# A token-major input replaced by a channel-major one in a hybrid mixer layer: no input transposes, norms by a column of ones, input loads on two queues

## The chip, the cores and the metric

The kernel runs on one core of a Trainium2 chip. That core has five engines, each with its own in-order instruction stream: TensorE (PE) for matrix products and transposes, VectorE (DVE) and ScalarE (ACT) for elementwise work and reductions, GpSimd (POOL), and SyncE (SP), which here only issues DMAs. ACT and POOL can issue DMAs too. The metric is device microseconds of one execution, as the median of several runs; lower is better. In the profile an instruction is named by its engine and by the line of the kernel file that made it.

## The reference

One layer reads 128 context tokens and 512 latent tokens of 1024 channels. The part that the change touches comes first in the layer: every token is divided by its root mean square, scaled and shifted by an adaLN modulation that depends on the group (context or latent), and sent through one input projection of 3840 columns.

```python
shift, scale, gate = jnp.split(silu(c) @ w_ada + b_ada, 3)
h = x * rsqrt(mean(x * x, -1) + EPS) * g_pre * (1 + scale) + shift
proj = h @ w_in            # 3840 columns: attention, HGRN2, Fourier, gates
```

The rest of the layer (neighbourhood attention with a position bias, a two-way gated linear recurrence, a Fourier mixing branch, the gates, the output projection, the post-norm and the residual) is the same before and after.

## The kernel before

All arithmetic is fp32. A large product is made from three fast ones: each operand is split into a rounded part `hi` and a remainder `lo` (`split`, line 129), and `mm3` (line 210) adds hi·hi, hi·lo and lo·hi in one PSUM bank. The 640 tokens (128 context, then 512 latent) are columns, handled in two halves of 320; the 1024 channels are eight groups `k` of 128, which lie on the partitions of `hT[0]` and `hT[1]` (the `hi` and the `lo` part of the modulated input `h`).

The start (`start_stream`, line 244) works like this. `load_x` (line 217) loads the input token-major: for each of five blocks of 128 tokens one tile `xa` of 640 channels and one tile `xb` of 384, ten DMAs on SP. `scale_x` (line 222) sums the squares of each token (ACT for `xa`, DVE for `xb`), takes square root and reciprocal, and multiplies both tiles by the result. Then comes a loop over the channel groups. For each `k`, `mod_cols` (line 195) multiplies two 512 KB blocks of the modulation weights `wss`, one for the scale and one for the shift, by the SiLU of the conditioning vectors (`csil`, line 171). The result is copied to `row` (line 266), transposed (line 270) and reduced to the columns `G` and `shift` (lines 272 to 275). `modulated` (line 233) then transposes the five 128x128 blocks of `x` that belong to channel group `k` on TensorE, lets ACT read them from PSUM with `G` as scale and `shift` as bias (lines 237 and 239), and lets DVE make the `hi` and `lo` parts (lines 240 and 241). `zf_stream` (line 283) follows with the twelve matmuls of that `k` for the first two projection blocks `zf0` and `zf1`; when all eight are in, `gate` (line 321) takes sigmoids on ACT.

What follows is one long sequence of projection blocks (`FILL`, line 30), the first of which is `zb0`, and in between the recurrences, the attentions, the Fourier branch and the output projection. A small planner (`Order`, line 39) interleaves these streams at trace time by estimated times, and a scheduler fixes each engine's order from that. SP's weight loads are chained: `load_raw` (line 175) and `load` (line 190) queue each behind the last weight load. `lb` and `lb1` (lines 153 to 160) are constants of the recurrence gate, computed before everything else, with an exponential on ACT. `sel` (line 147) is a constant that the output gates need late.

Of the kernel before, what the change touches and what calls it, by code (L numbers as in the profile page):

```python
# [71 lines left out]
def mixer_kernel(ctx: ExitStack, tc: tile.TileContext, A, O):  # L72
# [51 lines left out]

    def tr(out, src):
        od.now += 0.107
        last_tr[0] = te.transpose(out, src, ident).ins  # L127

    def split(src, hi, lo, hi_eng=None, lo_eng=None):
        (sc.copy if hi_eng is None else hi_eng.tensor_copy)(hi, src)  # L130
        (ve if lo_eng is None else lo_eng).tensor_sub(lo, src, hi.bitcast(F32))  # L131
# [19 lines left out]


    lb, lb1 = const("lb", [2, 2]), const("lb1", [2, 2])
    ve.tensor_sub(lb, lbl, lbl)
    sc.activation(lb, lb, ACT.Exp)
    ve.reciprocal(lb1, lb)
    ve.tensor_mul(lb, lb, lb1)
    ve.tensor_sub(lb, lb, lb)
    ve.tensor_scalar_max(lb, lb, 0.0)
    ve.tensor_scalar(lb1, lb, -1.0, 1.0, op0=ALU.mult, op1=ALU.add)  # L160
# [12 lines left out]
    wdma, nb = [], [1]  # L173
# [7 lines left out]
    def split_w(raw, lo_eng=None, shape=(KT, P), tags=("hi", "lo")):  # L181
        hi, lo = [wp.tile([P, *shape], F32R, tag=t, name=nm(t), bufs=WB[t]) for t in tags]
        split(raw, hi, lo, lo_eng=lo_eng)
# [11 lines left out]
    def mod_cols(out, w, chain):  # L195
# [8 lines left out]
    xa, xb = [T(tag="xa") for _ in range(5)], [T(384, tag="xb") for _ in range(5)]  # L204

    def xcols(i, k):
        return (xa[i] if k < 5 else xb[i])[:, k % 5 * P:k % 5 * P + P]
# [14 lines left out]
    def scale_x():  # L222
        for i in range(5):
            ss2 = S(2)
            sc.activation(T(), xa[i], ACT.Square, accum_out=ss2[:, 0:1])
            ve.tensor_tensor_reduce(PE_()[:, 0:384], xb[i], xb[i], 1.0, 0.0, op0=ALU.mult, op1=ALU.add,
                                    accum_out=ss2[:, 1:2])
            ve.tensor_add(rstd[:, i:i + 1], ss2[:, 0:1], ss2[:, 1:2])
# [902 lines left out]
```

## Time and profile before

| what | value |
|---|---|
| median of 3 runs (lowest to highest) | 435.74 us (435.19 to 435.88) |
| the profiled execution's own time | 436.31 us |
| its span, from first to last instruction | 434.5 us |
| busy PE / DVE / ACT / POOL | 410.3 / 303.2 / 204.7 / 7.4 us |
| instructions | 8311 |
| first matmul starts | 14.27 us |
| the chain that ended last: share on PE | 90% |

Busy time is the sum of the instructions' spans on an engine. Matmuls are pipelined, so two of them may overlap in a row of the timeline: the distance between two starts is what one costs, not its printed length. A row such as "idle before, releaser" says how long the engine sat idle just before an instruction and what ended that. The matmuls of `mod_cols` show as two records each, so one 512 KB block of modulation weights is x16 in the trace. "Slices" are fortieths of the span.

### The profile page before, as it was taken

Reading aid. Unit: us, or ns where it says so; the run is one execution under the profiler, and the core shown is the slowest. Engines: PE = TensorE matmul, PEld = TensorE weight load, DVE = VectorE, ACT = ScalarE, POOL = GpSimd, SP = SyncE. Lnnn points to the kernel's source line nnn. Section 1 sums busy time; section 2 is a strip of 40 time slices with the busy share of each in tenths; the row PEclk is TensorE's granted clock in tenths of the full one; section 3 lists DMA queues with packets and bytes.
Section 4 is the critical chain, followed back from the end, with each engine's and each line's share of the span. In section 5 each row is a group of like instructions: output and inputs, shape, how many; then the busy total and the mean of one; then the engine's idle time right before and its main releaser. Section 6 shows DMA issues by size and latency. Waiting matters only on the chain.

```text
span 434.5 us, 8311 instructions
## 1 busy us (share of the span) xinstructions
PE 410.3 (94%) x3176; PEld 373.0 (86%) x3176; DVE 303.2 (70%) x866; ACT 204.7 (47%) x546; POOL 7.4 (2%) x23
## 2 busy tenths in 40 slices
PE   0699999999998999999999999999999999999994
PEld 0388899999988998999899989899898889988884
DVE  2775479999986865885597658786679748471164
ACT  5524467575341525654454534744456553251231
POOL 2000000000020100000000000000000000000000
PEclk9999999999999999999999999999999999999999
DMA  7996143211202011132112423245324203245032
GB/s 241 411 407 228 49 154 116 66 55 50 84 23 74 13 60 50 56 97 66 40 61 67 146 67 92 93 152 181 100 55 141 98 1 105 76 160 205 0 146 98
DMA packets 19528, 47.62 MB, mean 110 GB/s; under 512 B 3184, under 2 KB 6912, under 8 KB 19488
## 3 DMA queue, kind: packets, MB, share of 16 engines
q1 hardware_dynamic: 19376, 46.94, 31.7%
q8 instruction: 25, 0.41, 0.4%
q0 software_dynamic: 112, 0.14, 0.3%
q14 instruction: 15, 0.12, 0.1%
HBM read 43.80 MB, written 3.28 MB: 108 GB/s over the span
## 4 chain that ended last, share of the span: by engine, by line
PE 90%; DVE 4%; DMA 3%; ACT 1%; issue 1%; SPq 0%; DVEq 0%; ACTq 0%
PE pb L113 83%; PE pb L127 6%; DMA vs<-wss 1%; DMA txa<-x 1%; DVE AL L451 1%; DVE t L525 1%; DVE AL L488 0%; ACT L681 0%; DVE lo L131 0%; DVE t L953 0%; ACT hi L130 0%; ACT pe L682 0%; DVE t L468 0%; DVE t L467 0%; DVE AC L451 0%
## 5 line engine op out<-in xcount | busy, mean ns | idle before, releaser
L113 PE MATMUL pb<-hT,hi 128*128 128x320 f32 x896 | 209.5, 317 | 3.0 <-DVE vs L131 1.5
L113 PEld LDWEIGHTS pb<-hT,hi 128*128 128x128 f32 x896 | 149.4, 188 | 9.5 <-issue 2.3
L113 PE MATMUL pb<-hT,lo 128*128 128x320 f32 x448 | 139.0, 312 | 0.0
L113 PEld LDWEIGHTS pb<-hT,lo 128*128 128x128 f32 x448 | 84.1, 188 | 1.0 <-DVE G L274 0.2
L131 DVE TENSOR_TENSOR lo<-raw,hi 128x1024 fp32r<-128x1024 f32 x35 | 42.8, 1223 | 26.9 <-ACT hi L130 26.5
L130 ACT CAST hi<-raw 128x1024 fp32r<-128x1024 f32 x35 | 36.8, 1051 | 41.9 <-PE pb L113 20.9
L113 PE MATMUL pb<-t,t 64*128 64x128 f32 (+2 forms) x414 | 43.1, 291 | 0.4 <-DVE AL L451 0.4
L113 PEld LDWEIGHTS pb<-t,t 64*128 64x128 f32 (+1 forms) x414 | 36.2, 188 | 4.8 <-issue 0.8
L130 ACT CAST pT<-pb 128x256 fp32r<-128x256 f32 x64 | 23.3, 372 | 19.3 <-DVE pT L131 12.3
L113 PE MATMUL pb<-hi,mh 128*128 128x512 f32 (+1 forms) x108 | 32.1, 376 | 0.0
L131 DVE TENSOR_TENSOR pT<-pb,pT 128x256 fp32r<-128x256 f32 x64 | 26.4, 418 | 1.7 <-ACT pT L130 1.5
L113 PEld LDWEIGHTS pb<-hi,mh 128*128 128x128 f32 x108 | 19.4, 189 | 3.2
L113 PE MATMUL pb<-pT,mh 128*128 128x512 f32 (+1 forms) x102 | 22.2, 364 | 0.0
L681 ACT ACTIVATE pe<-pb,s 128x256 f32<-128x256 f32 x32 | 15.3, 477 | 13.8 <-DVE s L680 7.9
L127 PE MATMUL pb<-ident,pe 128*128 128x128 f32 x136 | 20.9, 273 | 0.5 <-ACT pe L682 0.5
L113 PEld LDWEIGHTS pb<-pT,mh 128*128 128x128 f32 x102 | 17.7, 189 | 3.1
L936 ACT ACTIVATE t<-pb 128x512 f32<-128x512 f32 (+1 forms) x11 | 6.0, 551 | 30.1 <-PE pb L113 30.1
L113 PE MATMUL pb<-lo,mh 128*128 128x512 f32 (+1 forms) x54 | 20.2, 373 | 0.0
L127 PEld LDWEIGHTS pb<-ident,pe 128*128 128x128 f32 x136 | 16.6, 140 | 1.4 <-ACT pe L682 0.7
L451 DVE COPY_PREDICATED AL<-masks,pb 128x512 f32<-128x512 uint32 x24 | 16.5, 738 | 1.5 <-PE pb L113 1.5
L113 PE MATMUL pb<-pT,vs 128*128 128x256 f32 (+1 forms) x96 | 16.8, 321 | 0.0
L113 PE MATMUL pb<-vs,csil 128*32 128x128 f32 x64 | 3.3, 335 | 14.3 <-DMA vs<-wss 14.3
(205 smaller groups left out, 636.3 us busy)
## 6 DMA issues: line engine op xcount, KB each, us to landing
raw<-win SPq DMA_DIRECT2D x30, 512.0 KB, 3.5
pT<-wss SPq DMA_DIRECT2D x12, 512.0 KB, 10.2
raw<-wg SPq DMA_DIRECT2D x8, 512.0 KB, 3.5
raw<-wout SPq DMA_DIRECT2D x8, 512.0 KB, 3.5
t<-x SPq DMA_DIRECT2D x10, 256.0 KB, 6.1
o_y<-t SPq DMA_DIRECT2D x9, 256.0 KB, 2.1
vs<-wss SPq DMA_DIRECT2D x4, 512.0 KB, 9.3
tbl<-tbl SPq DMA_DIRECT2D x4, 512.0 KB, 3.5
```

Of the source, the lines that this page charges most:

```text
L113: return te.matmul(out, lhsT, rhs, start=start, stop=stop).ins
L127: last_tr[0] = te.transpose(out, src, ident).ins
L130: (sc.copy if hi_eng is None else hi_eng.tensor_copy)(hi, src)
L131: (ve if lo_eng is None else lo_eng).tensor_sub(lo, src, hi.bitcast(F32))
L451: ve.copy_predicated(out, mk.to_broadcast([P, i1 - i0, P]), src)
L525: ve.scalar_tensor_tensor(sall[r, cdst], sall[r, cs], Td[r, ip:ip + 1], pst[r, cdst], op0=ALU.mult, op1=ALU.add)
L681: sc.activation(pe[:, 256:512], ss[:, 256:512], ACT.Exp, bias=m[:, 1:2], accum_out=m[:, 3:4])
L936: sc.activation(T(512)[:, cs], po[:, 0:cs.stop - cs.start], ACT.Square, accum_out=ssb[:, j:j + 1])
```

## The change

The input gets a second layout in memory, `xT`: channels on the partitions, all 640 tokens along the free dimension, eight tiles of 128x640.

- Loads. The ten loads of `xa` and `xb` on SP go. Eight loads of `xT` tiles come, the even ones on SP and the odd ones on ACT's queue, as the first DMAs of the kernel. The conditioning vectors `cc` move from SP's front to ACT's queue, behind its four tiles; `lbl` moves to ACT's queue as well; `sel` moves from POOL's queue to SP's chain of loads, behind the weight loads of the first groups. The first weight load is now chained behind SP's last `xT` tile.
- Norms. ACT squares each `xT` tile and DVE adds the eight squares up. Five matmuls with a two-column block of ones add over the partitions, which leaves each token's sum on its partition. One square root and one reciprocal for all tokens follow, then five transposes of the result broadcast along a row, and two ACT copies: `rb` holds the inverse norm of every token on every partition. DVE multiplies each `xT` tile by `rb`, one tile per channel group.
- Modulation. The forty 128x128 transposes of `x` go; ACT reads the scaled `xT` tile from SBUF.
- Order. Edges (`turn`, `turn_names`) fix the order of some instructions on one engine: the modulation matmuls of group k+1 behind the row transposes of group k, DVE's `row` copy behind the last modulation step of the group before (for the first two groups behind its `lo` part of `hT`), the next multiplication by `rb` behind that copy, and the first weight splits behind `rb` and behind the first `h`.
- `lb` and `lb1` are computed after the `zf` matmuls, with their exponential behind the last `h` on ACT.

```diff
-    cc = const("cc", [KT, 2], dma=sy.dma_start)
-    lbl = const("lbl", [2, 2], dma=sy.dma_start)
+    xT = []
+    for k in range(KT):
+        xT.append(T(tag="xT"))
+        x_dma = (sc if k % 2 else sy).dma_start(xT[k], A["xT"][k]).ins
+        if k % 2 == 0:
+            x_last = x_dma
+    cc = const("cc", [KT, 2], dma=sc.dma_start)
...
-    sel = const("sel", [2, P])
+    ones = cp.tile([P, 2], F32, tag="ones", name="ones")
+    ve.memset(ones, 1.0)
...
-    wdma, nb = [], [1]
+    wdma, nb = [x_last], [1]
...
+            if k == 0 and prev is not None:
+                turn_names(chain[0], prev)
...
-    def load_x():
-        for i in range(5):
-            load(xa[i], A["x"][i * P:(i + 1) * P, 0:NT])
-            load(xb[i], A["x"][i * P:(i + 1) * P, NT:D])
-    def scale_x(): ...
+    def inverse_norms():
+        acc = T()
+        sc.activation(acc, xT[0], ACT.Square)
+        for k in range(1, KT):
+            sq = T()
+            sc.activation(sq, xT[k], ACT.Square)
+            ve.tensor_add(acc, acc, sq)
+        pn, pr = PB(), PB()
         for i in range(5):
+            mm(pn[:, 2 * i:2 * i + 2], acc[:, i * P:(i + 1) * P], ones)
+        sc.activation(rstd, pn[:, 0:10].rearrange(...)[:, :, 0], ACT.Sqrt, bias=eps, scale=1.0 / D)
+        ve.reciprocal(rstd, rstd)
+        for i in range(5):
+            tr((pr if i < 4 else pn)[:, i % 4 * P:i % 4 * P + P], rstd[:, i:i + 1].to_broadcast([P, P]))
+        rb = T()
+        sc.copy(rb[:, 0:512], pr)
+        return rb, sc.copy(rb[:, 512:NT], pn[:, 0:P])
-    def modulated(k, pm):
-        h, px = T(), PB()
-        for i in range(1, 5):
-            tr(px[:, (i - 1) * P:i * P], xcols(i, k))
-        sc.activation(h[:, P:NT], px, ACT.Identity, bias=shift[:, k, 1:2], scale=G[:, k, 1:2])
-        tr(pm[:, 384:512], xcols(0, k))
-        sc.activation(h[:, 0:P], pm[:, 384:512], ACT.Identity, bias=shift[:, k, 0:1], scale=G[:, k, 0:1])
+    def modulated(k):
+        h = T()
+        sc.activation(h[:, P:NT], xT[k][:, P:NT], ACT.Identity, bias=shift[:, k, 1:2], scale=G[:, k, 1:2])
+        h_act[0] = sc.activation(h[:, 0:P], xT[k][:, 0:P], ACT.Identity, bias=shift[:, k, 0:1], scale=G[:, k, 0:1])
...
-        scale_x()
+        rb, rb_act = inverse_norms()
+        ve.tensor_mul(xT[0], xT[0], rb)
...
-                mod_cols(pm[:, u * P:(u + 1) * P], raws[2 * k + u], [])
+                mod_cols(pm[:, u * P:(u + 1) * P], raws[2 * k + u], [], row_tr)
             yield 0
-            ve.tensor_copy(row, pm[:, 0:256])
+            row_copy = ve.tensor_copy(row, pm[:, 0:256])
+            if k:
+                turn(row_copy, row_done)
+            if k + 1 < KT:
+                turn(ve.tensor_mul(xT[k + 1], xT[k + 1], rb), row_copy)
...
+            row_tr = last_tr[0]
...
-            ve.tensor_scalar_add(shift[:, k, :], pt[:, 2:4], bss[:, k, 1:2])
-            modulated(k, pm)
+            row_done = ve.tensor_scalar_add(shift[:, k, :], pt[:, 2:4], bss[:, k, 1:2])
+            h_done = modulated(k)
             if k < 2:
-                zf_w.append(split_w(zraw[k]))
+                row_done = h_done
+            if k < 2:
+                zf_w.append(split_w(zraw[k], prev=rb_act))
+                rb_act = h_act[0]
...
+    lbl = const("lbl", [2, 2], dma=sc.dma_start)
+    def lower_bounds():
+        ve.tensor_sub(lb, lbl, lbl)
+        turn(sc.activation(lb, lb, ACT.Exp), h_act[0])
...
         for p in range(2):
             for u in range(2):
                 gate(p, 0, zf_acc[p][u][:, 0:320], u)
...
     def gate_vectors():
+        sel = const("sel", [2, P], dma=load)
```

In `zf_stream`, `lower_bounds()` is called between the last `zf` matmul and the four calls of `gate` shown above. On the host, `xT` is the transpose of `x`, cut into eight tiles; `x` itself stays as an input, since the residual at the end reads it.

More of the change, by code (lines that the diff above doesn't have):

```diff
@@ L123, in run_mm, with turn_names, turn @@
         chain.append(ins)
+    def turn_names(ins, prev):
+        tc.add_manual_dep(ins, prev.name, mybir.DependencyInfo(mybir.DependencyClass.NoSync, mybir.DependencyReason.DATA),
+                          reason="turns")
+    def turn(ins, prev):
+        turn_names(ins.ins, prev.ins)
+        return ins
     def tr(out, src):
@@ L127, in tr, with split @@
         last_tr[0] = te.transpose(out, src, ident).ins
-    def split(src, hi, lo, hi_eng=None, lo_eng=None):
-        (sc.copy if hi_eng is None else hi_eng.tensor_copy)(hi, src)
+    def split(src, hi, lo, hi_eng=None, lo_eng=None, prev=None):
+        ins = (sc.copy if hi_eng is None else hi_eng.tensor_copy)(hi, src)
+        if prev is not None:
+            turn(ins, prev)
         (ve if lo_eng is None else lo_eng).tensor_sub(lo, src, hi.bitcast(F32))
@@ L150, in mixer_kernel @@
     ve.memset(eps, EPS)
[L153 to L160, printed above, removed]
     def rsqrt_mean(ss, n):
@@ L179, in load_raw, with split_w @@
         return t
-    def split_w(raw, lo_eng=None, shape=(KT, P), tags=("hi", "lo")):
+    def split_w(raw, lo_eng=None, shape=(KT, P), tags=("hi", "lo"), prev=None):
         hi, lo = [wp.tile([P, *shape], F32R, tag=t, name=nm(t), bufs=WB[t]) for t in tags]
-        split(raw, hi, lo, lo_eng=lo_eng)
+        split(raw, hi, lo, lo_eng=lo_eng, prev=prev)
         return hi, lo
@@ L193, in load, with mod_cols @@
             sy.dma_start(t, src)
-    def mod_cols(out, w, chain):
+    def mod_cols(out, w, chain, prev=None):
         t = od.now
@@ L203, in mixer_kernel @@
     hT = [big.tile([P, KT, NT], F32R, tag=f"hT{j}", name=f"hT{j}") for j in range(2)]
-    xa, xb = [T(tag="xa") for _ in range(5)], [T(384, tag="xb") for _ in range(5)]
-    def xcols(i, k):
-        return (xa[i] if k < 5 else xb[i])[:, k % 5 * P:k % 5 * P + P]
     zf_w, zf_acc = [], [[PB("f"), PB("f")], [PB("f"), PB()]]
@@ L215, in mixer_kernel @@
     HF = (slice(0, 320), slice(320, 640))
-    def load_x():
+    def inverse_norms():
[6 more added lines that the diff above has]
+        pn, pr = PB(), PB()
         for i in range(5):
-            load(xa[i], A["x"][i * P:(i + 1) * P, 0:NT])
-            load(xb[i], A["x"][i * P:(i + 1) * P, NT:D])
-    def scale_x():
+            mm(pn[:, 2 * i:2 * i + 2], acc[:, i * P:(i + 1) * P], ones)
+        sc.activation(rstd, pn[:, 0:10].rearrange("p (i two) -> p i two", two=2)[:, :, 0], ACT.Sqrt, bias=eps, scale=1.0 / D)
+        ve.reciprocal(rstd, rstd)
@@ L223, in scale_x @@
         for i in range(5):
[L224 to L228, printed above, removed]
-            rsqrt_mean(rstd[:, i:i + 1], D)
-            ve.tensor_scalar(xa[i], xa[i], rstd[:, i:i + 1], 0.0, op0=ALU.mult, op1=ALU.add)
@@ L281, in start_stream @@
             yield max(0.0, 13.5 + 2.7 * (k + 1) - od.now)
+    lb, lb1 = const("lb", [2, 2]), const("lb1", [2, 2])
+    lbl = const("lbl", [2, 2], dma=sc.dma_start)
+    def lower_bounds():
+        ve.tensor_sub(lb, lbl, lbl)
+        turn(sc.activation(lb, lb, ACT.Exp), h_act[0])
+        ve.reciprocal(lb1, lb)
+        ve.tensor_mul(lb, lb, lb1)
+        ve.tensor_sub(lb, lb, lb)
+        ve.tensor_scalar_max(lb, lb, 0.0)
+        ve.tensor_scalar(lb1, lb, -1.0, 1.0, op0=ALU.mult, op1=ALU.add)
     def zf_stream():
@@ L290, in zf_stream @@
                 yield 0
+        lower_bounds()
         for p in range(2):
```

7 lines of the change are left out of this document (4 added, 3 removed).

## The prediction

> **What bounds the kernel now.** I read the page's busy shares first, then the waits of PE, then the busy time by stage, then the timeline of the first 55 us engine by engine.
>
> ```profile
> PE 410.3 (94%) x3176; PEld 373.0 (86%) x3176; DVE 303.2 (70%) x866; ACT 204.7 (47%) x546; POOL 7.4 (2%) x23
> ```
>
> The waits of PE over the whole span (us, times, longest), and the busy time by stage (stretch, its length, then busy time of PE, PEld, DVE, ACT, POOL with counts, the granted clock, the DMA engines' share, GB/s):
>
> ```profile
> PE pb L113 <- DMA vs<-wss: 14.3, 1, 14.3
> PE pb L113 <- DVE vs L131: 1.5, 1, 1.5
> PE pb L113 <- ACT t L326: 1.0, 1, 1.0
> ...
> 14.27:21.77 7.50, 7.30 (x75) 4.30 (x75) 5.09 (x17) 3.15 (x5) 0.00 (x0) 1.00 1.03 409
> ...
> 24.20:52.65 28.45, 28.45 (x337) 25.82 (x335) 16.29 (x49) 10.06 (x16) 0.00 (x0) 1.00 0.58 225
> ...
> 53.81:429.64 375.83, 371.99 (x2744) 340.99 (x2744) 271.57 (x767) 180.93 (x504) 4.33 (x12) 1.00 0.27 87
> ```
>
> PE waits once for 14.3 us, for its first weights, and then hardly at all: 372.0 of 375.8 us busy after the start. So whatever moves the instant 52.65, at which PE has finished the start's work, moves the rest rigidly; the change edits only what comes before it (and `sel` and `lb`, below). What fills PE from the first matmul on `h` (21.77, which I call T0) to 52.65:
>
> ```profile
> L113 PE MATMUL pb<-hT,hi 128*128 128x320 f32 x80 | 19.3, 327 | 0.1
> L113 PE MATMUL pb<-hT,lo 128*128 128x320 f32 x40 | 12.0, 314 | 0.0
> L113 PE MATMUL pb<-pT,csil 128*32 128x128 f32 x146 | 5.6, 277 | 0.0
> L127 PE MATMUL pb<-ident,txa 128*128 128x128 f32 x16 | 2.9, 283 | 0.0
> L127 PE MATMUL pb<-ident,row 128*128 128x128 f32 x14 | 2.8, 280 | 0.0
> L127 PE MATMUL pb<-ident,txb 128*128 128x128 f32 x15 | 2.5, 276 | 0.0
> L113 PE MATMUL pb<-vs,csil 128*32 128x128 f32 x48 | 2.2, 307 | 0.0
> ```
>
> Their real cost is the distance between starts (timeline of PE):
>
> ```profile
> 19.37 1.33 PE L127 MATMUL pb<-ident,txa 128*128 128x128 f32 x5
> 20.63 1.08 PE L113 MATMUL pb<-pT,csil 128*32 128x128 f32 x16
> 21.77 1.17 PE L113 MATMUL pb<-hT,hi 128*128 128x320 f32 x3
> ...
> 24.54 0.30 PE L113 MATMUL pb<-hT,lo 128*128 128x320 f32 x1
> 24.68 0.31 PE L113 MATMUL pb<-hT,hi 128*128 128x320 f32 x1
> ...
> 27.14 1.08 PE L113 MATMUL pb<-pT,csil 128*32 128x128 f32 x32
> 28.15 0.76 PE L127 MATMUL pb<-ident,txa 128*128 128x128 f32 x5
> ```
>
> From 24.5 on a 320-column matmul costs 0.147 us (24.54 to 24.68 and so on), five transposes about 0.73 (0.147 each), and the modulation of a whole group (x32) 1.01 us. Before that, all three cost about twice as much: one half of a group's modulation (x16) takes from 20.63 to 21.7, five transposes 1.26. So 120 x 0.147 = 17.6 us on `hT`, six groups of modulation 6.1, fourteen row transposes 2.1, thirty-one input transposes 4.6: 30.4 of the 30.9 us, the rest being the slow first pieces.
>
> **What goes.** Thirty-one of the forty input transposes lie in that full stretch: 4.6 us of PE, with nothing else to hide them. The other nine lie before T0, where PE is mostly waiting for the chain. DVE loses `scale_x`, ACT its five squares.
>
> **What T0 becomes.** Now the norms of all tokens hang on the last `xT` tile. The rows that bear on its arrival and on each link:
>
> ```profile
> 0.73 0.39 SPq L140 DMA_DIRECT2D cc<-cc  x1
> 1.65 0.42 SPq L193 DMA_DIRECT2D txa<-x  x1
> ...
> 2.00:10.70 8.70, 0.00 (x0) 0.00 (x0) 2.90 (x14) 4.90 (x11) 1.92 (x5) 1.00 0.93 293
> 6.00:7.00 1.00, 0.00 (x0) 0.00 (x0) 0.03 (x2) 0.00 (x0) 0.00 (x0) 1.00 1.01 272
> 10.00:36.00 26.00, 21.53 (x266) 16.28 (x267) 18.17 (x59) 10.80 (x23) 0.00 (x0) 1.00 1.03 407
> ...
> L541 ACT ACTIVATE t<-t 128x640 f32<-128x640 f32 x2 | 1.5, 737 | 0.1
> L424 DVE TENSOR_TENSOR t<-t,t 128x640 f32<-128x640 f32 x2 | 1.6, 818 | 0.0
> L113 PE MATMUL pb<-bones,t 128*128 128x2 f32 x20 | 2.5, 248 | 0.0
> L164 ACT ACTIVATE rstd<-rstd,eps 128x1 f32<-128x1 f32 x5 | 1.4, 288 | 1.3 <-DVE rstd L228 1.3
> L501 ACT COPY t<-pb 128x512 f32<-128x512 f32 x4 | 2.1, 589 | 8.3 <-PE pb L127 8.3
> L237 ACT ACTIVATE t<-pb,shift,G 128x512 f32<-128x512 f32 x8 | 6.2, 779 | 17.4 <-DVE G L274 17.4
> ...
> 21.22 0.49 DVE L240 CAST hT<-t 128x640 fp32r<-128x640 f32 x1 [1.60 <-ACT t L239]
> ```
>
> The ten loads are 2.62 MB (640 x 1024 x 4 bytes); at the 293 GB/s of the stretch they are in at about 10.9. The first `xT` load can be issued where `cc` was, at 0.73 instead of 1.65, 0.9 us earlier, with the same bytes: last tile at about 10.2 (with its receipt). Bounds: from 2.1 on, 407 GB/s would give 8.5 and 272 GB/s 11.7. Then: square 0.74; last add 0.82; five ones-matmuls, by the `bones` rows 0.63 and at the early pace twice that, 1.2; square root 0.29, its table load (1.28 elsewhere) behind add and matmuls; reciprocal 0.16; five transposes at the early pace 1.33; ACT copies 0.59 and about 0.3; multiplication 0.82; `h` in two ACT pieces 1.1; cast 0.49. Sum 7.8; with nine handoffs at 0.07 (the cast of 21.22 ends at 21.71, its matmul starts at 21.77) 8.5: T0 = 18.7. PE is in order and the first modulation weights land meanwhile, so one group at the early pace (two x16, 2.1 us) may stand between these small steps; I add 1.0. **T0 = 19.7**, bounds 17.0 (tiles at 8.5, nothing in between) and 25 (the first rival).
>
> On DMA a rule of the skill speaks against part of the change. The two-queue issue gets nothing from me but the 0.9 us start, because with one queue issuing the engines were already full (row 6.00 to 7.00 above: a share of 1.01).
>
> The Trainium skill, "DMA: Bandwidth & Descriptors", section "Issuing engines are not separate DMA queues", says that DMAs started by different engines run on the same 16 DMA engines and that only the time to issue is saved. The trace agrees as far as it goes; if the rule were wrong and two queues reached the 407 GB/s of later, the sum would gain 1.7 us.
>
> **From T0 to the end of the stage.** PE then has 17.6 + 6.1 + 2.1 = 25.8 us of work. Two things come on top. The early slow pace: it ended 2.4 us after T0 (24.2); I take 3 us at half speed, 1.5 us (bounds 0.5 and 4). And holes: the new edges make DVE's `row` copy of group 1 wait for `lo` of group 0, and put modulation k+1 behind row transposes k, so from group 2 on DVE paces the groups:
>
> ```profile
> L241 DVE TENSOR_TENSOR hT<-t,hT 128x640 fp32r<-128x640 f32 x8 | 6.6, 823 | 0.2
> L131 DVE TENSOR_TENSOR lo<-raw,hi 128x1024 fp32r<-128x1024 f32 x3 | 3.7, 1220 | 0.1
> L266 DVE COPY row<-pb 128x256 f32<-128x256 f32 x8 | 3.4, 421 | 1.6 <-PE pb L113 1.6
> L273 DVE TENSOR_SCALAR G<-s,bss 128x2 f32<-128x2 f32 x8 | 1.8, 227 | 0.2
> L272 DVE TENSOR_REDUCE s<-pb 128x4 f32<-128x16 f32 x8 | 1.4, 172 | 5.9 <-PE pb L127 5.9
> ```
>
> Back to back each starts about 0.08 before its printed end of the one before, so a group is 0.34 copy + 0.74 new multiplication + 0.10 reduce + 3 x 0.14 + 0.41 cast + 0.74 `lo` = 2.75 us. PE per group: 1.01 + 0.29 + 12 x 0.147 = 3.06. The two nearly balance, so holes come only near group 1, whose whole chain (copy, transposes, `G`, `h`, cast, `lo`) takes 4.8 us from T0 with 3 to 4 us of PE work to fill it: 1.5 us (bounds 0 and 3). End of the stage = T0 + 28.8 = 48.5, against 52.65: **4.1 us gained**. Weights do not bind: input, sixteen modulation blocks and two projection blocks are 12.1 MB, of which 2.55 were in at 10.7 and the rest follows at 407 GB/s, to 34 before and 33 after; the last group's chain behind them takes some 7 us, to 40.
>
> **What is moved.** `cc` arrives at about 10 instead of 3 us; its only reader is the SiLU for modulation, which needs weights that land later, unless ACT's order makes others wait (first rival). The exponential of `lb` with its own table goes from ACT's first idle microseconds to between the last `h` and the sigmoids:
>
> ```profile
> 0.73 1.28 ACT L155 ACT_TABLE_LOAD   x1 [0.73 <-PEq L1124]
> ...
> 51.70 1.28 ACT L325 ACT_TABLE_LOAD   x1 [2.08 <-PE pb L113]
> ```
>
> ACT sat idle 2.08 us there, which covers 1.28 + 0.2; uncovered it would cost up to 1.5. The sigmoids' own load, and with it PE's 1.0 us wait, stays. `sel` (128 KB) joins SP's chain, 0.3 us of DMA where weights are ahead of PE; `lbl` is 2 KB; memset, ones and DVE's seven adds (0.82 each) lie in the wait for the tiles. All of this I cost at nothing.
>
> Against the profiled execution's 436.31 us (434.5 us of span and 1.8 around it) this gives 432.2; the median of the runs is 0.57 lower, so **431.6 us**.
>
> **The rivals.** All but the last are priced by end = T0 + 28.8; T0 = 23.9 gives no gain at all.
>
> *ACT's queue blocks the norms (slower).* `cc` is issued fifth on ACT behind 1.3 MB of tiles. If the scheduler puts its SiLU ahead of the squares, ACT sits until about 10.4, then needs eight squares at about 0.65 apart before the last add: 15.6 instead of 10.9, T0 = 24.4; and all modulation from group 2 on hangs behind T0 by the new edges, so that nothing is done ahead meanwhile. The end is 53.2, with holes of 3 us 54.7: 436.3 to 437.8, taken at 437. For: ACT ran this SiLU before its first square in the trace. Against: the tiles land one by one, so squares are ready first. If only some squares stand behind, T0 is about 22 and the time 434.
>
> *DVE takes over.* If in-order waits add 1.0 us to its 2.75, the groups come 3.75 us apart: 4.8 for group 1, five more groups 18.8, two weight splits 2.3, and 4.9 from the last `row` copy to the last `zf` matmul make T0 + 30.8 = 50.5: 433.6. For: DVE's chain has no slack once it paces. Against: DVE was busy 16.3 of 28.45 us there, and the addition is 8 x 0.74.
>
> *The slow pace lasts.* PE has less to do before T0, and before, the fast pace came only 10 us after the first matmul although PE was busy 7.30 of 7.50 us. If it comes 8 us after T0, 4 instead of 1.5 us are lost: 434.1. The Trainium skill, "TensorE: Matmul & The Clock Gate", Part 1, says that the array runs at half clock until a busy window of about 3.4 us has passed. The trace agrees with the factor of two, not with the time: 24.5 is 10 us after the first matmul.
>
> *Everything goes well.* Tiles at 8.5, nothing between the small steps, no holes, an early pace that ends after 1 us: T0 = 17.0, end 43.3, 426.4; with half of that, 429.0.
>
> **How the numbers follow.** Forecast (429.0 to 433.5) 0.56; more gain 0.06; slow pace or DVE 0.14 (to 434.5); part of the squares blocked 0.09, of which a third is no change; norms blocked altogether 0.15, of which 0.03 within 0.2% and 0.12 slower. About 0.2% (0.9 us) is what a measurement can tell from no change. Faster 0.82, same 0.06, slower 0.12. For 8 in 10 the range is 428.8 to 435.4.
>
> **What would show it.** First matmul on `hT` near 19.7; no transposes of the input; the multiplications by `rb` at 0.82 us; PE full from about 24 to 48.5; the sigmoids' table load near 47.5; from there all rows 4 us earlier and the same. Wrong if squares start after 10 us, if T0 is past 23.9, if PE shows long waits between groups 1 and 3, or if later stages lose what the start gains (their order on the engines is set by the same scheduler, and I take it as unchanged).

## The result, and the profile after

The changed kernel is slower: 440.55 us in the median (439.01 to 441.72, 4 runs) against 435.47 (434.78 to 435.88) for the kernel before on the same chip, a ratio of 1.012 with an interval of 1.010 to 1.014. The forecast was 431.6, range 428.8 to 435.4. Measured a second time (below) it took 439.18, a ratio of 1.008; the two intervals do not overlap, and what made the first occasion slower by another 1.4 us is not known. Both are slower, where the forecast was faster. The profiled execution of the changed kernel took 439.01 us, with a span of 437.0; everything below is read from it against the profiled 436.31 and 434.5 of before.

The busy row of the page of the changed kernel, and the row of its PE matmuls on `bones`, a matmul far behind the start, with first and last start at the end of the row:

```profile
PE 408.7 (94%) x3151; PEld 372.7 (85%) x3151; DVE 306.7 (70%) x853; ACT 206.3 (47%) x542; POOL 7.6 (2%) x22
```

```profile
L113 PE MATMUL pb<-bones,t x20: 168/251/272, 122.8 to 146.0; 128*128 128x2 f32 x20
```

The same row of the kernel before:

```profile
L113 PE MATMUL pb<-bones,t x20: 168/251/272, 120.7 to 144.0; 128*128 128x2 f32 x20
```

PE has 1.6 us less to do and yet comes to `bones` 2.1 us later, and to its last matmul 2.04 us later (430.33 against 428.29). So the difference that the two profiles show arises ahead of this row, and the rest is shifted rigidly, as forecast, only in the other direction. (The spans of the profiles differ by 2.5 us, the medians by 5.1 and 3.5; the first experiment takes this up.) Span less first `bones` row is 313.8 us before and 314.2 after, and it lies between 313.8 and 314.4 in every run of this study. This row therefore serves as the mark of lateness below.

The waits of PE in the first 60 us of the changed kernel (us, times, longest), and the busy time by stage (stretch, length, busy time of PE, PEld, DVE, ACT, POOL with counts, granted clock, DMA share, GB/s):

```profile
PE pb L113 <- DVE t L230: 13.9, 1, 13.9
...
PE pb L113 <- DVE hT L248: 2.7, 3, 1.1
...
PE pb L136 <- DVE row L275: 1.9, 2, 1.3
```

```profile
24.53:29.06 4.53, 4.53 (x45) 3.94 (x45) 3.68 (x8) 0.59 (x2) 0.00 (x0) 1.00 0.66 261
29.06:45.07 16.01, 13.41 (x212) 10.82 (x209) 13.32 (x36) 6.27 (x11) 0.00 (x0) 1.00 0.74 272
...
54.80:430.00 375.20, 372.45 (x2750) 341.64 (x2750) 271.03 (x765) 181.21 (x503) 5.00 (x12) 1.00 0.26 87
```

PE's long first wait no longer ends with its first weights but with DVE's last addition of squares (L230). After T0 = 24.53, where the first product on `hT` starts (21.77 before), PE has holes: 13.41 of 16.01 us busy up to 45.07, where before it was full. From 54.8 on it is as full as before.

The chain from the last input tile to T0, with DVE's first six additions ahead of it, from the timeline of the changed kernel (start, length, engine, line, instruction, in brackets the idle time before it and what ended that):

```profile
7.09 5.48 DVE L230 TENSOR_TENSOR t<-t,t 128x640 f32<-128x640 f32 x6 [6.20 <-ACT t L229]
...
11.57 0.74 ACT L229 ACTIVATE t<-txT 128x640 f32<-128x640 f32 x1 [0.77 <-DMA txT<-xT]
...
12.89 0.16 DVE L305 TENSOR_TENSOR lb<-lbl 128x4 f32<-128x4 f32 x1 [0.32 <-DMA lbl<-lbl]
12.97 0.82 DVE L230 TENSOR_TENSOR t<-t,t 128x640 f32<-128x640 f32 x1
...
13.85 2.30 PE L113 MATMUL pb<-ones,t 128*128 128x2 f32 x10 [13.85 <-DVE t L230]
16.19 0.27 ACT L234 ACTIVATE rstd<-pb,eps 128x5 f32<-128x5 f32 x1 [2.58 <-PE pb L113]
...
16.82 1.30 PE L136 MATMUL pb<-ident,rstd 128*128 128x128 f32 x5 [0.67 <-DVE rstd L235]
...
18.05 1.08 PE L113 MATMUL pb<-vs,csil 128*32 128x128 f32 x16
...
18.73 0.83 DVE L264 TENSOR_TENSOR txT<-txT,t 128x640 f32<-128x640 f32 x1 [2.06 <-ACT t L240]
...
19.68 1.23 DVE L142 TENSOR_TENSOR lo<-raw,hi 128x1024 fp32r<-128x1024 f32 x1
20.82 0.42 DVE L275 COPY row<-pb 128x256 f32<-128x256 f32 x1
...
21.29 0.69 PE L136 MATMUL pb<-ident,row 128*128 128x128 f32 x2 [1.31 <-DVE row L275]
...
22.50 0.23 DVE L288 TENSOR_SCALAR G<-G,gpre 128x2 f32<-128x2 f32 x1
22.76 0.81 ACT L246 ACTIVATE t<-txT,shift,G 128x512 f32<-128x512 f32 x1 [3.11 <-DVE G L288]
...
23.99 0.49 DVE L248 CAST hT<-t 128x640 fp32r<-128x640 f32 x1 [1.26 <-ACT t L247]
24.53 1.70 PE L113 MATMUL pb<-hT,hi 128*128 128x320 f32 x5 [0.69 <-DVE hT L248]
```

Two chains stand one behind the other here that could run side by side. The norms need the last tile, ones, square root, transposes, copies and the scaling (done at 19.56). The modulation of group 0 needs only its weights and `csil`; but on PE its matmuls stand behind the norms' transposes, at 18.05, and its `row` copy on DVE stands behind a weight split (19.68). So `G` is ready only at 22.73, 3.2 us after the scaled tile, and ACT sits 3.11 us for it.

### The profile page after: what moved, and what is told of

Read it like the earlier page. It is cut to its first block, busy times and chain, and to the rows that moved or that the text cites. A ratio compares the mean times of both kernels' runs of the same rounds, so it can differ in the third digit from the quotient of the medians.

```text
span 437.0 us, 8244 instructions
## 1 busy us (share of the span) xinstructions
PE 408.7 (94%) x3151; PEld 372.7 (85%) x3151; DVE 306.7 (70%) x853; ACT 206.3 (47%) x542; POOL 7.6 (2%) x22
## 4 chain that ended last, share of the span: by engine, by line
PE 87%; DVE 4%; DMA 4%; ACT 3%; issue 1%; SPq 0%; DVEq 0%; ACTq 0%
PE pb L113 82%; PE pb L136 5%; DMA lbl<-lbl 2%; DMA raw<-win 2%; DVE lo L142 1%; DMA txT<-xT 1%; ACT hi L139 1%; DVE t L556 1%; SPq L186 0%; ACT L712 0%; DVE AL L482 0%; DVE t L985 0%; ACT pe L713 0%; ACT t L532 0%; DVE t L499 0%
## 5 line engine op out<-in xcount | busy, mean ns | idle before, releaser
L713 ACT ACTIVATE pe<-m,s 128x256 f32<-128x256 f32 x32 | 16.2, 505 | 0.0
```

The source lines that it names most:

```text
L713: sc.activation(pe[:, 0:256], sb, ACT.Exp, bias=m[:, 1:2], accum_out=m[:, 2:3])
```

## The experiments

One table first; the columns are T0 (the first product on `hT`), the first start of the `bones` row and the span of the profiled execution, then the median of the timed runs and the ratio to the kernel before, which was measured on the same chip (its median there was 435.27 to 435.67; the row "before" is the first measurement).

| run | T0 | bones | span | median | ratio (95%) |
|---|---|---|---|---|---|
| before | 21.77 | 120.7 | 434.5 | 435.47 | |
| changed | 24.53 | 122.8 | 437.0 | 440.55 | 1.0118 (1.0100 to 1.0136) |
| changed, again | 24.66 | 123.4 | 437.6 | 439.18 | 1.0080 (1.0065 to 1.0095) |
| modulation 0 first | 21.93 | 121.3 | 435.5 | 437.37 | 1.0039 (1.0022 to 1.0056) |
| changed, PE busy early | 23.56 | 124.5 | 438.7 | 439.13 | 1.0083 (1.0060 to 1.0107) |
| before, PE busy early | 21.63 | 120.8 | 434.6 | 436.38 | 1.0019 (1.0007 to 1.0032) |
| changed, no edges | 30.67 | 126.2 | 440.4 | 441.74 | 1.0153 (1.0138 to 1.0168) |
| before, two queues | 21.14 | 119.5 | 433.6 | 435.80 | 1.0015 (1.0005 to 1.0024) |
| changed, no norms | 18.31 | 116.3 | 430.5 | 432.42 | 0.9940 (0.9925 to 0.9955) |
| three orders mended | 21.80 | 120.1 | 434.3 | 436.85 | 1.0031 (1.0020 to 1.0043) |
| broadcast sums | 26.45 | 124.8 | 439.0 | 441.47 | 1.0154 (1.0131 to 1.0176) |
| sums in one bank | 23.60 | 125.1 | 439.4 | 440.93 | 1.0129 (1.0112 to 1.0146) |
| logarithm and exponential | 19.19 | 118.2 | 432.5 | 434.68 | 0.9982 (0.9974 to 0.9991) |
| the same, filled | 19.76 | 119.7 | 434.1 | 435.44 | 0.9993 (0.9982 to 1.0004) |

**The changed kernel again.** Nothing is changed. Expected:

> The changed kernel itself once more, for the spread of its time. Theory (the pace): the timed runs of the changed kernel lie 2 to 5 us above what its profiled execution shows (437.0 us of span), because PE is left idle so often in the first 45 us that its fast pace comes at a different instant in each execution, or is lost again; then this profile shows a start of the fast pace other than 29 us, and a total lag over the kernel before of 2 to 5 us that is complete before 60 us. Rival (the rest of the kernel): the additional microseconds are lost later, after 60 us; then the lag at 60 us is 2 us again and grows behind it.

It is slower again, by 3.5 us. Of these the profiles show 2.6 (the `bones` row, 123.4 against 120.7); the profiled execution of before was itself 0.8 us above the median of its runs. The 2 to 5 us that the expectation wanted to explain did not come back: the four executions lie between 438.85 and 439.47, the profiled one at the upper end. So it decides neither case.

**The modulation of group 0 ahead of the norms.**

```diff
-        rb, rb_act = inverse_norms()
-        ve.tensor_mul(xT[0], xT[0], rb)
...
-                mod_cols(pm[:, u * P:(u + 1) * P], raws[2 * k + u], [], row_tr)
+                mods = []
+                mod_cols(pm[:, u * P:(u + 1) * P], raws[2 * k + u], mods, row_tr)
+            if k == 0:
+                rb, rb_act = inverse_norms(mods[-1])
+                ve.tensor_mul(xT[0], xT[0], rb)
...
-            mm(pn[:, 2 * i:2 * i + 2], acc[:, i * P:(i + 1) * P], ones)
+            m = mm(pn[:, 2 * i:2 * i + 2], acc[:, i * P:(i + 1) * P], ones)
+            if i == 0:
+                turn_names(m, after)
```

> The modulation matmuls of channel group 0 go ahead of the five ones-matmuls on PE; row copy, transposes and G of group 0 then fall into the norms' waits. Nothing else is changed. Theory (order): the first h was late (22.76 us) because PE did group 0's modulation only behind the norm transposes (18.05), so that G came 3.2 us after the scaled tile; then h of group 0 starts at about 19.7, the first matmul on hT at about 21.5 to 22 instead of 24.53, and the time falls by about 2.5 to 3 us, to no more than the kernel before. Rival (norm chain): the scaled tile is what h waits for, and moving the modulation ahead only delays the norms by what PE does first; then the first matmul on hT stays at 24 or later and the time stays the same.

PE in its timeline:

```profile
11.10 1.08 PE L113 MATMUL pb<-vs,csil 128*32 128x128 f32 x16 [11.10 <-DMA vs<-wss]
12.49 1.08 PE L113 MATMUL pb<-pT,csil 128*32 128x128 f32 x16 [0.31 <-DMA pT<-wss]
13.96 2.30 PE L113 MATMUL pb<-ones,t 128*128 128x2 f32 x10 [0.39 <-DVE t L230]
...
21.93 1.43 PE L113 MATMUL pb<-hT,hi 128*128 128x320 f32 x4 [1.90 <-DVE hT L250]
```

The weights were there at 11.1 and 12.5, so in the changed kernel both halves of the modulation waited for nothing but PE's order. T0 comes 2.6 us earlier, as expected; the time falls by 1.8 us against the second measurement of the changed kernel, not by 2.5 to 3, and stays 0.4% above the kernel before. Half of the loss is this order. Behind T0 a part is given back: from T0 to `bones` it is 99.3 us here, 98.2 in the changed kernel, and DVE's second weight split (21.80, 1.22 long) now stands ahead of the `lo` part of group 0. The ones-matmuls still take 2.30 us.

**PE kept busy early, in both kernels.** 46 transposes of the identity, into a bank that nobody reads, ahead of PE's first useful matmul; the same lines in the kernel before.

```diff
+NWARM = 46
...
+    warm = PB()
+    chain = []
+    for i in range(NWARM):
+        ins = te.transpose(warm[:, i % 4 * P:i % 4 * P + P], ident, ident).ins
+        if chain:
+            turn_names(ins, chain[-1])
+        chain.append(ins)
```

> The changed kernel with 46 transposes of the identity matrix on PE before its first useful matmul, from about 3.5 to 13.5 us; nothing reads their result. Theory (the pace): PE's pace doubles only after a stretch of dense work, and the change has removed the dense work from the start; then ones-matmuls, norm transposes and modulation run at half their time (2.30 to 1.2, 1.30 to 0.7, 1.9 to 1.0 us), the first matmul on hT is at about 21.5, no matmul on hT takes 0.27 us, and the time falls by 5 us or more, below the kernel before. Rival (the pace is not bought by dummy work, or does not last over the gaps at 16 to 21 us): no more than 1 us is gained.

> The kernel before with the same 46 transposes of the identity ahead of its first useful matmul. Theory (the pace): its start is slow for the same reason, from 14.27 to 24.2 us; at the double pace the pieces before its first matmul on hT (21.77) shrink by 2 to 3 us, and the time falls by 2 to 4 us. If it gains as much as the changed kernel does from them, the pace does not explain the difference between the two; the theory needs the changed kernel to gain at least 1.5 us more. Rival: its start is bound by the arrival of weights and by DVE, and it gains less than 1 us.

Neither gained. In the changed kernel the transposes ran from 3.21 to 10.71, and the ones-matmuls then took 1.47 instead of 2.30 us; but PE had waited 3.06 us before them, and the granted clock, the share of its full clock that PE was given, fell (stretches of 2 us; the granted clock is the third number from the end):

```profile
12.00:14.00 2.00, 0.23 (x2) 0.23 (x3) 1.24 (x3) 1.50 (x2) 0.00 (x0) 1.00 1.00 399
14.00:16.00 2.00, 1.42 (x11) 1.33 (x11) 0.19 (x1) 0.27 (x1) 0.00 (x0) 0.68 1.05 418
16.00:18.00 2.00, 2.00 (x25) 1.61 (x28) 0.24 (x1) 1.03 (x3) 0.00 (x0) 0.50 1.01 401
...
42.00:44.00 2.00, 2.00 (x15) 1.84 (x8) 2.00 (x6) 0.00 (x0) 0.00 (x0) 0.50 0.42 166
```

It stayed at 0.50 until 28.4, and fell again at 42, after another wait of 2.36 us. In the kernel before PE waited 4.15 us for its weights behind the transposes, and the clock was at 0.50 from 15.1 to 18.5. An early pace was of no use to a PE that then had to wait.

**The edges taken out.** Every `turn` goes through `turn_names`, so all of them are gone.

```diff
     def turn_names(ins, prev):
-        tc.add_manual_dep(ins, prev.name, ..., reason="turns")
+        return
```

> The changed kernel without its order edges (turn and turn_names do nothing); the scheduler orders everything by its own estimates. Theory (the edges make holes): PE waited 2.7 us for hT and 1.9 us for row copies because modulation k+1 is held behind the row transposes of group k and the row copies behind DVE's other work; then without the edges these waits shrink to under 2 us in all and the time falls by 1 to 3 us. Rival (the edges are needed): without them DVE multiplies many tiles by the inverse norms ahead of the first hT cast, the first matmul on hT comes later than 24.5 us, and the time rises by 1 to 4 us.

The rival of that expectation was right. Without the edges DVE multiplies seven tiles in a row, and `row` of group 0 stands behind them:

```profile
21.53 5.43 DVE L278 TENSOR_TENSOR txT<-txT,t 128x640 f32<-128x640 f32 x7
...
27.35 1.12 PE L135 MATMUL pb<-ident,row 128*128 128x128 f32 x4 [5.51 <-DVE row L274]
...
30.67 1.43 PE L113 MATMUL pb<-hT,hi 128*128 128x320 f32 x4 [2.20 <-DVE hT L247]
```

In the profiles the edges are worth 2.8 to 3.4 us of span (440.4 against 437.6 and 437.0), in the ratios 0.35 to 0.7%; it is not they that make the change slow.

**Two queues, in the kernel before.**

```diff
-            load(xb[i], A["x"][i * P:(i + 1) * P, NT:D])
+            sc.dma_start(xb[i], A["x"][i * P:(i + 1) * P, NT:D])
```

> The kernel before with only the loads changed: the five xb tiles are issued on ACT's queue, the five xa tiles stay on SP. Theory (the same engines move the data): the first modulation weights land within 1 us of 14.27 as before, and the time stays within 1 us. Rival (two queues load faster, and that carries over): the first matmul comes 1 us or more earlier and the time falls by as much. A second rival: ACT's issues and the loads' competition with the weights delay the first norms, and the time rises by 1 us or more.

PE's first weights land 1.1 us earlier (13.16 instead of 14.27), the `bones` row 1.2 us earlier in the profile, but the median is 435.80 against 435.29 of before beside it: no gain that can be measured, rather a loss of 0.15%. The first half of the rival came true, the earlier first matmul, and the second did not. In the forecast the two queues got only the 0.9 us of the earlier start. The Trainium skill, "DMA: Bandwidth & Descriptors", section "Issuing engines are not separate DMA queues", says that DMAs issued by several engines run on the same 16 DMA engines and that only the time of issuing is saved. The medians agree with that, but the transfers did run faster here, 314 GB/s from 2.00 to 8.00 us against 244 before; whether issuing earlier explains all of this, the run does not show.

**The norms left out.** `rb` is a tile of ones; squares, sums, square root and transposes are gone, the scaling stays.

```diff
-        ...
-        sc.copy(rb[:, 0:512], pr)
-        return rb, sc.copy(rb[:, 512:NT], pn[:, 0:P])
+        ve.memset(rb, 1.0)
+        return rb, sc.copy(rb[:, 0:2], ones)
```

> The changed kernel without the norms: squares, sums, ones-matmuls, root and the transposes of the inverse norms are left out, and the tiles are multiplied by ones, so the input is not normalised. It measures what the chain of the norms costs. Theory (the norm chain and what PE does behind it set the first h): the first matmul on hT comes at 17 to 18.5 us instead of 24.5, and the time falls by 5 to 7 us below the changed kernel, to 2 to 4 us below the kernel before. Rival (the later part of the start binds by itself: DVE's groups, waits for weights): the first matmul on hT comes just as early, but less than 3 us of it reaches the end.

Without the chain of the norms T0 is 18.31, and `bones` comes 6.5 us earlier than in the changed kernel, for 6.2 us at T0: 1 to 1. The kernel is then 0.6% faster than before, so the second half of the forecast (no input transposes, all else rigid) holds in its direction, and the norms, with what stands behind them, turn 0.6% faster into 0.8 to 1.2% slower. With all other orders as they are here, no better chain of norms can bring more than this: about 432.4 us.

**Three orders mended.** The modulation first, as above; the first weight split no longer behind `rb`; the subtraction of `lbl` on DVE behind the last group's `lo` part.

```diff
-        ve.tensor_sub(lb, lbl, lbl)
+        turn(ve.tensor_sub(lb, lbl, lbl), h_last[0])
...
-                zf_w.append(split_w(zraw[k], prev=rb_act))
+                zf_w.append(split_w(zraw[k], prev=rb_act if k else None))
```

> As the run with the modulation of group 0 ahead of the norms, and two more edits of order: the split of the first projection weights is no longer held behind the inverse norms (ACT has idle time before), and the subtraction for lb waits behind the last group instead of standing in DVE's order ahead of the last add. Theory: the last add comes 0.6 us earlier, ACT's 1.06 us rounding leaves the path to the first h, and DVE's two 1.22 us remainders no longer stand ahead of the first hT; the first matmul on hT is at 19.5 to 20.5 instead of 21.93, and the time falls by 1 to 2 us below that run, to the kernel before or just below it. Rival: the slow pace and the waits behind group 0 eat it, and the time stays within 0.5 us of that run.

436.85 us: 0.5 us below the run with the modulation alone, near the rival of the expectation, and still 0.3% above before. T0 is that of before (21.80), not 19.5 to 20.5. ACT took the freed weight split first, waited for its weights, and loaded the table of the square root only behind it (with the modulation alone, at 12.38):

```profile
14.32 1.04 ACT L139 CAST hi<-raw 128x1024 fp32r<-128x1024 f32 x1 [1.71 <-DMA raw<-win]
15.38 1.28 ACT L236 ACT_TABLE_LOAD   x1
...
16.68 0.27 ACT L236 ACTIVATE rstd<-pb,eps 128x5 f32<-128x5 f32 x1
```

So the square root starts at 16.68 instead of 16.30, and a part of what remains is order again. The profiled execution was 0.7 us below the median of this run, that of before 0.8 above its own: the two profiles, with nearly the same span, cannot show where the 1.6 us between the medians lie.

**Sums broadcast by a matrix of ones.** No DVE additions, no transposes: 16 accumulating matmuls of 320 columns put the sum on every partition; square root and reciprocal there.

```diff
-            ve.tensor_add(acc, acc, sq)
...
+            for u in range(2):
+                mm(pn[u][:, 0:320], onesr, sq[:, HF[u]], start=(k == 0), stop=(k == KT - 1))
...
+        for u in range(2):
+            sc.activation(rb[:, HF[u]], pn[u][:, 0:320], ACT.Sqrt, bias=eps, scale=1.0 / D)
+            ve.reciprocal(rb[:, HF[u]], rb[:, HF[u]])
```

> Starts from the run with the modulation of group 0 ahead of the norms, the first weights split not held back, and the lower-bound subtraction moved behind the last group. Now the norms are formed without VectorE additions and without transposes: ScalarE squares each input tile as before, and TensorE multiplies each square with a 128x128 matrix of ones, 16 matmuls of 320 columns that accumulate over the 8 tiles, so that the sum over the channels stands in every partition at once; a square root and a reciprocal of 2x320 columns give the factor. Theory (the start of the full-rate work is set by the chain additions -> sums -> square root -> transposes -> copies -> scaling -> first product, and the rest follows it rigidly): the eight additions' tail, the 1.3 us of transposes and the two copies go, a longer square root and reciprocal come; the first product that uses the normalised input starts at 18.0 to 20.0 us instead of 21.8, and the time is 433 to 435.5 us, about 0.2 to 0.5% under the kernel before. Rival (the start is no longer what sets the end; half-rate TensorE time and late weights are): the first product starts earlier but the end does not follow, time 436 to 437.5. Third: the reciprocal of 320 columns costs so much more than that of 5 (0.19 us) that nothing is won at the start: first product at 21 us or later, time 436 to 438.

The third case, and worse than it said. DVE's reciprocal of 320 columns (group of its line, first 32 us):

```profile
L239 DVE RECIPROCAL t<-t 128x320 f32<-128x320 f32 x2 | 4.3, 2144 | 1.8 <-ACT t L238 1.8
```

6.7 ns a column, where the multiplication of 640 columns takes 0.82 us, 1.3 ns a column. The two stand ahead of `row`, `G` comes late, PE waits 3.69 us for `row` and 3.46 us for `hT`, and the granted clock is at 0.50 from 18.6 to 32.2.

**Sums in one bank.** Five matmuls of 10 columns per tile, 40 in all, add up in one accumulator; seven tiles of them ahead of the first modulation weights.

```diff
...
+            for i in range(5):
+                mm(pn[:, 0:10], sq[:, i * P:(i + 1) * P], onesr[:, i, :], start=(k == 0 and i == 0), stop=(k == KT - 1 and i == 4))
...
```

> Starts from the run with the modulation of group 0 ahead of the norms and the lower-bound subtraction moved behind the last group. The sums of squares of the 8 tiles are no longer added on VectorE: TensorE adds them as they come, five matmuls of 10 columns for each tile into one accumulator, seven tiles of them while TensorE would otherwise wait for the first modulation weights. The square root's table is loaded early by a one-element square root, the first high part is cast between the square root and the copies, and the scaling of the second tile and the low part of the first block come behind the first product's operand. The reciprocal is the short one of 5 columns again (0.19 us instead of the 2x2.15 us of the run with the broadcast sum). Theory (the late start and nothing else sets the end, and the late norm chain sets the start): factor copied at about 16 us instead of 19.1, first product that uses the input at 18.5 to 20 us instead of 21.8, row of the bones 1.5 to 3 us earlier than 120.1, time 433.5 to 435.5 us. Rival (an earlier start is given back, because the modulation weights and the half-rate stretch then hold the groups up): first product 1.5 to 3 us earlier, bones less than 1 us earlier, time 436 to 437.5 us.

Neither case. PE in the timeline of this run, and then its busy time and granted clock by stretch:

```profile
7.87 7.63 PE L113 MATMUL pb<-onesr,t 128*128 128x10 f32 x35 [7.87 <-ACT t L236]
...
15.43 1.08 PE L113 MATMUL pb<-vs,csil 128*32 128x128 f32 x16
```

```profile
24.00:26.00 2.00, 1.51 (x6) 0.88 (x4) 2.00 (x3) 0.00 (x0) 0.00 (x0) 0.66 1.02 403
26.00:28.00 2.00, 1.60 (x12) 1.21 (x16) 2.00 (x4) 0.00 (x0) 0.00 (x0) 0.50 0.70 279
...
34.00:36.00 2.00, 2.00 (x37) 1.53 (x36) 0.99 (x5) 0.87 (x2) 0.00 (x0) 0.78 1.03 422
```

35 matmuls of only 10 columns took 7.63 us, 0.22 each, almost as much as 320 columns cost with the broadcast sums (16 in 3.92 us, 0.25 each), so the modulation started at 15.43 instead of 11.7. And though T0 is only 1.8 us later than with the orders mended, `bones` is 5.0 us later: after a wait of 1.79 us before T0 the granted clock went to 0.50 for 10.2 us (24.6 to 34.9).

**Logarithm and exponential.** The broadcast sums again, seven tiles of them ahead of the modulation; the factor as exp(-0.5 ln(mean + eps)) on ACT. The lines taken out below are those of the run with the broadcast sums.

```diff
-            sc.activation(rb[:, HF[u]], pn[u][:, 0:320], ACT.Sqrt, bias=eps, scale=1.0 / D)
-            ve.reciprocal(rb[:, HF[u]], rb[:, HF[u]])
+            sc.activation(rb[:, HF[u]], sums[u][:, 0:320], ACT.Ln, bias=eps, scale=1.0 / D)
+        for u in range(2):
+            act = sc.activation(rb[:, HF[u]], rb[:, HF[u]], ACT.Exp, scale=-0.5)
...
```

> The sums of squares again as in the run with the broadcast sum (two matmuls of 320 columns with a 128x128 matrix of ones for each tile, so that every partition has the sum), but seven of the eight tiles ahead of the first modulation weights, and the factor as exp(-0.5 ln(mean + eps)) on ScalarE, 2x2 instructions of 320 columns, in place of the square root and the 2x2.15 us of reciprocals; no transposes and no copies. The modulation of group 0 comes ahead of the factor, its gain operations ahead of the first scaling on VectorE; the first low part of the weights is formed before the first product's operand is cast, the second scaling after it. Theory (the position of the whole start, not only of the first product, sets the end): the factor is ready at 15.5 to 17 us instead of 19.1 with the sums of 5 columns, first product at 18.5 to 20 us instead of 21.8, row of the bones at 117.5 to 119.5 instead of 120.1 us, time 433 to 435.5 us. Rival (the groups behind the first wait for weights and for the half-rate stretch): first product as early, but the operand of the second group no earlier than in the run this starts from and bones at 120 or later, time 436 to 438 us.

PE and ACT in its timeline:

```profile
7.95 4.47 PE L113 MATMUL pb<-t,t 128*128 128x320 f32 x14 [7.95 <-ACT t L236]
12.35 0.64 PE L113 MATMUL pb<-vs,csil 128*32 128x128 f32 x16
...
14.39 1.28 ACT L250 ACT_TABLE_LOAD   x1
...
15.69 0.83 ACT L250 ACTIVATE t<-t 128x320 f32<-128x320 f32 x2
...
19.19 1.50 PE L113 MATMUL pb<-hT,hi 128*128 128x320 f32 x3 [1.83 <-DVE hT L259]
```

All as in the theory: factor at 16.5, T0 19.19, `bones` 118.2, and 434.68 us against 435.39 of before beside it. This kernel beats both: the one before by 0.18%, the changed one by 1.0 to 1.3%. The orders mended had given 436.85, the sums with the reciprocal 441.47. But three things differ from the run with the reciprocal: the factor, the seven tiles ahead of the modulation, and some orders on DVE that the expectation lists. What each of them brings was not taken apart.

**The same, filled.** 16 transposes of the identity between the modulation of the second group and T0.

```diff
+            if k == 1:
+                for i in range(16):
+                    tr(sums[0][:, 0:P], ident)
```

> The run with the logarithm and the exponential, and nothing else changed than that 16 transposes of the identity, whose result nobody reads, stand on TensorE between the modulation of the second group (which ended at 17.36 us there) and the first product (19.19 us): 16 at 0.104 us, the pace of transposes at the full clock, fill 1.66 of the 1.83 us for which TensorE had been idle. Theory (it was this idle stretch, after TensorE had come to its full pace, that brought the granted clock down to 0.50 from 19.5 to 22.2 us): the rows of the granted clock stay at 1.00 between 18 and 24 us, the first products take 0.31 us from the start instead of 0.47, the row of the bones comes 0.5 to 1.5 us earlier than 118.2, time 433.2 to 434.3 instead of 434.7 us. Rival (the fall of the clock has another cause, or what it costs is hidden behind the operands of the second group): clock still at 0.50 there, or bones within 0.3 us of 118.2, time 434.4 to 435.0.

The granted clock in the run without the filling, and then with it:

```profile
18.00:20.00 2.00, 0.81 (x2) 0.50 (x2) 1.97 (x4) 1.54 (x3) 0.00 (x0) 0.75 1.02 406
20.00:22.00 2.00, 2.00 (x8) 1.91 (x8) 2.00 (x4) 0.00 (x0) 0.00 (x0) 0.50 1.02 401
```

```profile
20.00:22.00 2.00, 1.70 (x10) 1.14 (x9) 2.00 (x4) 0.12 (x1) 0.00 (x0) 1.00 1.00 388
...
28.00:30.00 2.00, 2.00 (x20) 1.58 (x23) 0.51 (x4) 0.00 (x0) 0.00 (x0) 0.50 1.03 410
```

Half right. The fall at 19.0 is gone, which fits the idle time before it as its cause; one execution does not prove it, since the full pace had also come at least 1 us later in this one (the modulation matmuls at 12.47 still took 1.0 us, those at 12.35 in the run without the filling 0.57). And after PE's next wait, 1.67 us for the second group at 25.93, the clock was at 0.50 from 27.2 to 30.5, where PE has work. T0 and `bones` come 0.6 and 1.5 us later (the rows before the filling are 0.57 us late already), the time is 435.44: no gain.

## Why the prediction was wrong, point by point

*That the rest is moved rigidly*: right from the `bones` row on, to 0.6 us over the profiles of all runs.

*T0 = 19.7*: wrong by 4.8 us, and this is the step that failed; the bounds (17 to 25) held it. Its terms, against the chain above. The last square ends at 12.31 instead of 10.9, inside the bounds that were given. The DMA engines were not slower than the 293 GB/s of the sum: from 4.00 to 11.57 they moved 401. (The share of 1.01 that the forecast read as full engines went with 272 GB/s, a share of 1.04 in this stretch with 401.) But the sum let the tiles run alone, and the first two blocks of modulation weights ran beside them, issued at 4.03 and 5.51 (8.31 and 8.82 before); by 11.57 some 3.7 MB were in, 1.0 more than the tiles. The last addition starts 0.66 us after its square. The forecast had costed the other additions and `lbl` at nothing; the additions start 0.93 us apart (six in 5.48 us), and the sixth of the seven kept DVE until 12.57; then `lbl` and its subtraction, ahead in DVE's order, took until 12.97. At that distance the last addition's turn came at 12.68, so that only about 0.3 us are `lbl`'s. The ones-matmuls take 2.3 instead of 1.2: the five are ten records in the trace, and the forecast counted five at the mean of the `bones` rows (2.5 us by 20). The steps from the square root to the scaling took 0.4 us less than summed. From the end of the scaling to T0 it is 4.97 instead of about 2.8: the forecast let the modulation weights land meanwhile and gave 1.0 us for PE's order, but that order put the modulation of group 0 behind the norms, and behind it came DVE's split, the copy, the row transposes and `G`: 2.2 us more, the largest miss of all the terms. The run with the modulation first gives 2.6 us of this back; without the norms T0 comes 6.2 us earlier.

*T0 to the end of the stage, 2.1 us less than before*: `bones` less T0 went from 98.96 to 98.23, so 0.7 less. Thirty-one transposes were taken at 0.147 us each, but five cost 0.52 at the full pace (in the kernel before, next start 28.67 after 28.15), 0.104 each, 3.2 us in all instead of 4.6. The holes were 2.6 us, not 1.5: waits of 0.99 and 1.05 us for `hT` and 0.55 for `row`. The half pace lasted until about 28.2, 3.7 us after T0, and cost some 1.8 instead of 1.5 (two row transposes took 0.56 us at 27.36, still at half pace; the 16 modulation matmuls at 27.92 took 0.59, where half pace is 1.0); in the kernel before it had ended by 23.95, where four transposes took 0.36 us, and not at 24.2. Against this PE's 1.0 us wait for the sigmoids' table, which was forecast to stay, is gone: both table loads, 51.42 and 52.94 in the timeline of ACT, are over before the gates. In part the holes look like lateness again, which no run tests: SP's weight loads are chained and wait for buffers that the late modulation frees (11.9 us of waits for PE in the first 40 us, 2.6 before), so that the first `zb0` weights were issued at 30.61 and landed at 37.57, and their split on DVE (38.65 to 39.87) stands right ahead of the cast for which PE waits 1.05 us.

*The rivals.* ACT's queue did not block the norms: `cc` was issued first (0.73), not fifth, and the squares began at 5.72. DVE did take over in part, before T0, where the additions, the subtraction of `lbl` and the split stood in the chain, and after it, where all three holes end with a row of DVE. The slow pace lasted 14 us from the first matmul, but only 3.7 us past T0, near the forecast's 3 and not the rival's 8. None of the three had the mechanism that decided, two independent chains in one order on PE; it stood in the forecast as 1.0 us.

*The rest*: nothing on the chain waits for `sel` or the memsets. ACT did wait for `cc` (until 4.30), and its SiLU with the table load stood ahead of the first square at 5.72; whether an earlier first square would have spared DVE's additions their lateness was not tested. What stays open: on the first occasion the unprofiled executions of the changed kernel were 1.5 to 2.7 us longer than the profiled one, on the second they were not. Their mean granted clock was 0.990 to 0.994, that of the profiled one 0.997; but an execution of the second occasion had 0.988 and was its shortest, so the clock is not shown to be the cause.

## What to carry to other kernels

When a reduction over a whole input is put ahead of the first use, add up the chain from its last tile to the first product link by link, and check in which order each in-order engine will take the other chain that meets it there; whatever can run while the tiles land should stand ahead of the reduction. Work taken from an engine is worth nothing if new waits take its place: 1.6 us of PE work went, and the product on `hT` came 2.8 us later. A start-to-start distance at the pace of the place, not a printed length, gives what an instruction costs, and a small matmul costs almost as much as one of 320 columns while the clock is slow.

## What the runs showed of the hardware that I had not expected

- Once PE had reached its full pace, waits of 1.67, 1.79, 1.83, 2.36, 3.06, 3.69 and 4.15 us came with a fall of the granted clock to 0.50, during the wait or up to 1.3 us after it; waits of 1.38 us (broadcast sums, at 42.16) and 1.52 us (the changed kernel again, at 41.01) did not. The Trainium skill, "TensorE: Matmul & The Clock Gate", Part 1, gives about 3.4 us of idleness for this; here half of it was enough; where the limit lies, these runs do not show.
- The stretches at 0.50, eight in the first 60 us of all runs, lasted 3.4 us (four of them), 10.2 (two) or 13.7 (two), that is one, three or four times the same length. Work did not end one early: with the logarithm PE was busy again from 19.19, and the clock stayed at 0.50 until 22.4.
- The full pace came 3.9 us after dense matmuls of 320 columns began with the broadcast sums (12.25 to 16.10), 4.4 us with the logarithm (7.95 to 12.35) and over 5 us in the same kernel filled (still half pace at 12.47, from 7.97), but not within 7.6 us of matmuls with 10 columns, and only 14 us after the first matmul in the changed kernel. The first slow stretch shows a granted clock of 1.00, only the later ones 0.50: the pace there has to be read from the distance of the starts.
- DVE's reciprocal takes 6.7 ns a column, five times a multiplication. It is cheap only on few columns (5 in 0.19 us).
